# The feed-forward products of an encoder layer as 2x2 blocks with seven block products

## The chip, the cores and the metric

The kernel runs on one core of a Trainium2 chip. The core has a matrix engine (TensorE, "PE" in the profile, with its weight loads as "PEld"), three engines for element work (VectorE "DVE", ScalarE "ACT", GpSimd "POOL"), and a sync engine ("SP") that issues nearly all DMA transfers here. Each engine works through its own instructions in order, and waits on semaphores for the others. PE reads its operands from SBUF and writes its sums to PSUM, which has room here for eight tiles of 128x512 float32 numbers. The metric is the device time of one execution in microseconds.

## The reference

One layer (DEPTH 1, 1024 tokens, D_MODEL 1024). Three token mixers feed gated projections, and the sum goes through `w_out`. After that comes the part that is changed:

```
x  = x + merged @ w_out                  # 1024x1024 @ 1024x1024
h2 = rms_norm(x, norm2_g)
x  = x + (silu(h2 @ ffn_w1) * (h2 @ ffn_w3)) @ ffn_w2
# D_FF = 2816: two products 1024x1024 @ 1024x2816, one 1024x2816 @ 2816x1024
```

All arithmetic is to have float32 accuracy.

## The kernel before

Every matrix operand is split into two parts, a high one of reduced precision ("hi", made by ScalarE with a type conversion) and the remainder ("lo", a subtraction on VectorE), see `split` (L90 to L92). A product is then three matmuls into the same PSUM tile, hi*hi, hi*lo and lo*hi, `mm3` (L94 to L97). Operands that come from DRAM go through `Prep` (L402 to L415): a DMA into a `wr` buffer, the hi part (L413) and the lo part (L414). These run under a raised priority `HP`: a planner in the framework orders the instructions of each engine when the program is built, from priorities and from times that it assumes, so the order of the code and the order on an engine can differ. That order is then fixed. Buffers come from pools: a `tag` has a number of slots, and a new tile waits until the tile that held the slot is no longer used. A pool that is opened where another was closed waits for the tiles that lay at its addresses.

The last third of the kernel has three parts.

The output projection (`out_proj`, L763) works on two halves of 512 tokens. In each it forms four column blocks of 256: per block 4 token tiles x 8 contraction tiles x 3 matmuls of 128x256, from the operand `mT` and prepared `w_out`; then VectorE adds the residual `xr` into `acc` (L777), which holds the whole of x in SBUF until the end. After four blocks, `norm_tile_T` (L417 to L429) computes the RMS norm of the half: ScalarE squares (L422), a short chain for the inverse root (L178 to L187), then for each token tile a scaling on VectorE (L426), 8 transposes on PE (L428) and a split of the transposed tile into h2T.

The feed-forward (`ffn`, L783) goes through 11 groups of 256 hidden columns. In a group, for two column tiles j and two token halves h, there are two PSUM tiles (w1 and w3) of 8 contraction tiles x 3 matmuls of 128x512; then Silu (L800), the product (L801) and a split into `gh`, `gl`, which stay in SBUF. The down projection of the group follows: 8 token tiles x 2 column halves x 2 contraction tiles x 3 matmuls, and VectorE adds each PSUM tile to `acc` (L813). Activations never leave SBUF. The weight buffers hold 2 raw and 8 split tiles.

The output is stored at the end of the last group, one DMA for each token tile.

## Time and profile before

| | |
|---|---|
| median of 3 runs | 2303.83 us (2302.22 to 2306.47) |
| the profiled execution's own time | 2300.59 us |
| its span (first to last instruction) | 2298.8 us |
| mean granted TensorE clock | 0.954 |
| PE busy | 2068.9 us (90%), 10929 matmuls |
| DVE busy | 1274.5 us (55%) |
| ACT busy | 798.4 us (35%) |
| POOL busy | 210.6 us (9%) |
| DMA | 278.51 MB, mean 121 GB/s |

Times within the trace count from the start of the span. The output projection begins at about 1441 us, the feed-forward at 1561 us, and the last result is added at 2294 us. A matmul's record lasts longer than the distance to the next matmul, because matmuls are pipelined: what one costs is the distance from start to start. The page names an idle stretch by the instruction that ended it.

### The profile page before, as it was taken

The numbers are of one execution on the slowest core, as the hardware profiler recorded it, in microseconds if no ns is written. First come the engines' busy times: TensorE is split into PE (matmuls) and PEld (weight loads), VectorE is DVE, ScalarE is ACT, GpSimd is POOL, SyncE is SP. The second block draws the span as 40 slices with busy tenths as digits, with TensorE's granted clock in tenths as the row PEclk, the third lists the DMA queues.
The fourth block names the chain that finished last, engine by engine and source line by source line (L and its number), as shares of the span: only waits on it lengthen the run. The fifth ranks groups of instructions, "written<-read, shape, count | busy, mean of one in ns | idle before, by whom it ended". The sixth has DMA issues, their size and how long they took to land.

```text
span 2298.8 us, 27560 instructions
## 1 busy us (share of the span) xinstructions
PE 2068.9 (90%) x10929; PEld 1735.1 (75%) x10929; DVE 1274.5 (55%) x1977; ACT 798.4 (35%) x1250; POOL 210.6 (9%) x123
## 2 busy tenths in 40 slices
PE   5488989979679998999998799989999999999999
...
PEclk8699999989889999999999999999999999999999
...
GB/s 182 93 208 172 202 143 218 197 248 167 184 169 238 185 174 115 117 67 133 123 137 86 163 84 138 196 114 23 33 55 55 55 37 56 55 27 48 55 19 74
DMA packets 120635, 278.51 MB, mean 121 GB/s; under 512 B 16518, under 2 KB 46712, under 8 KB 118970
## 3 DMA queue, kind: packets, MB, share of 16 engines
...
q0 software_dynamic: 512, 7.34, 0.9%
...
## 4 chain that ended last, share of the span: by engine, by line
PE 63%; DVE 15%; DMA 9%; ACT 6%; issue 3%; POOL 2%; SPq 1%; ACTq 0%; POOLq 0%; DVEq 0%
PE pf L97 11%; PE pf L96 11%; PE pf L95 11%; PE pT L95 4%; PE pT L96 4%; PE pT L97 4%; DVE wlo L414 2%; PE S L631 2%; DMA it<-iv 2%; DMA wraw<-in_w_out 1%; DMA ft<-fw 1%; PE T L645 1%; PE pm L95 1%; PE pm L96 1%; PE pm L97 1%
## 5 line engine op out<-in xcount | busy, mean ns | idle before, releaser
L413 ACT ACTIVATE whi<-wraw 128x512 fp32r<-128x512 f32 (+1 forms) x214 | 168.4, 794 | 476.4 <-PE pf L97 176.6
L414 DVE TENSOR_TENSOR wlo<-wraw,whi 128x512 fp32r<-128x512 f32 (+1 forms) x214 | 208.6, 982 | 222.9 <-ACT whi L413 215.5
L97 PE MATMUL pf<-h2T,wlo 128*128 128x512 f32 x704 | 280.4, 398 | 0.0
L96 PE MATMUL pf<-h2T,whi 128*128 128x512 f32 x704 | 277.8, 395 | 0.0
L95 PE MATMUL pf<-h2T,whi 128*128 128x512 f32 x704 | 276.4, 393 | 0.0
L95 PE MATMUL pT<-hT,whi 128*128 128x512 f32 x576 | 235.0, 408 | 14.0 <-DVE u L450 11.0
L96 PE MATMUL pT<-hT,whi 128*128 128x512 f32 x576 | 232.1, 403 | 0.8 <-DVE hT L92 0.8
L97 PE MATMUL pT<-hT,wlo 128*128 128x512 f32 x576 | 231.9, 403 | 0.0
L801 DVE TENSOR_TENSOR si<-si,pf 128x512 f32<-128x512 f32 x44 | 30.2, 687 | 306.1 <-PE pf L97 305.9
L95 PE MATMUL pN<-whi,hT 128*128 128x256 f32 x576 | 164.8, 287 | 14.0 <-DVE vl L92 8.1
L813 DVE TENSOR_TENSOR acc<-acc,pf 128x512 f32<-128x512 f32 x176 | 119.3, 687 | 96.7 <-PE pf L97 96.6
L96 PE MATMUL pN<-wlo,hT 128*128 128x256 f32 x576 | 164.8, 286 | 1.7 <-DVE wlo L414 1.7
L97 PE MATMUL pN<-whi,hT 128*128 128x256 f32 x576 | 164.1, 285 | 0.0
L96 PEld LDWEIGHTS pf<-h2T,whi 128*128 128x128 f32 x704 | 132.1, 188 | 33.9
L95 PEld LDWEIGHTS pf<-h2T,whi 128*128 128x128 f32 x704 | 132.3, 188 | 31.8
L97 PEld LDWEIGHTS pf<-h2T,wlo 128*128 128x128 f32 x704 | 132.2, 188 | 30.5
L95 PEld LDWEIGHTS pT<-hT,whi 128*128 128x128 f32 x576 | 110.8, 192 | 41.1 <-issue 11.0
L96 PE MATMUL pf<-wlo,gh 128*128 128x512 f32 x352 | 137.1, 390 | 0.0
L95 PE MATMUL pf<-whi,gh 128*128 128x512 f32 x352 | 137.1, 390 | 0.0
L97 PE MATMUL pf<-whi,gl 128*128 128x512 f32 x352 | 136.9, 389 | 0.0
L96 PEld LDWEIGHTS pT<-hT,whi 128*128 128x128 f32 x576 | 110.8, 192 | 26.0 <-DVE hT L92 1.3
L97 PEld LDWEIGHTS pT<-hT,wlo 128*128 128x128 f32 x576 | 110.4, 192 | 24.4 <-issue 0.2
...
## 6 DMA issues: line engine op xcount, KB each, us to landing
...
```

The lines of the kernel that those rows point to most:

```text
L95: nc.tensor.matmul(p,lh,rh,start=first,stop=False)
L96: nc.tensor.matmul(p,lh,rl,start=False,stop=False)
L97: nc.tensor.matmul(p,ll,rh,start=False,stop=last)
L413: nc.scalar.activation(hi,raw,AF.Identity)
L414: (self.lo_eng or nc.vector).tensor_tensor(lo,raw,hi.bitcast(F32),op=ALU.subtract)
L631: nc.tensor.matmul(S[:,512*n:512*n+512],q[:,c,128*t:128*t+128],k[i][:,c,512*n:512*n+512],start=i==0,stop=i==1)
L645: for i in range(4): nc.tensor.transpose(T[:,i,:],e[:,512*n+128*i:512*n+128*i+128],E.ident)
L801: V.tensor_tensor(si,si,P[1],op=ALU.mult)
L813: V.tensor_tensor(acc[:,t,512*d:512*d+512],acc[:,t,512*d:512*d+512],p,op=ALU.add)
```

## The change

The up projection is computed on 2x2 blocks. The normed tokens are cut into two halves of tokens and two halves of the contraction, A11, A12, A21, A22; the weight columns into tile i and tile 11+i and the same two halves of the contraction, B11, B12, B21, B22. With S1=A21+A22, S2=S1-A11, S3=A11-A21, S4=A12-S2, and T1=B12-B11, T2=B22-T1, T3=B22-B12, T4=T2-B21, the four result blocks come from seven block products A11*B11, A12*B21, S4*B22, A22*T4, S1*T1, S2*T2, S3*T3 and seven additions, instead of eight products. This is done for w1 and w3 side by side: a pair of PSUM tiles per product, 2 x 4 contraction tiles x 3 matmuls = 24 matmuls of 128x512.

- `out_proj` loads x into `acc` (now 512 tokens, two slots, of which one becomes `raw0`, the unsplit transposed first half), squares each block as it is done, stores the residual to DRAM (`E.res`), and in the second half forms S1 to S4 and A22 in place of a plain split. The S tiles (`ms`) take the place of `mT`. Between the last block and the second norm, `meanwhile` puts the first two block products of the first group.
- `ffn_up` runs 11 iterations. Each loads four weight tiles, forms T1 to T4 on VectorE, splits seven weight tiles, and combines the PSUM pairs on VectorE and ScalarE into C11, C12, C21, C22. From the gated activations g11, g12, g21, g22 GpSimd forms s1 to s4, and seven 256 KB tiles are stored to DRAM (`E.gs`).
- `ffn_down` runs seven jobs, one for each block product of the down projection. A job goes through 11 contraction tiles in six spans: it loads the activation operand from `E.gs`, splits it, forms the weight combination in place where there is one, splits that, and runs 4 token tiles x 3 matmuls for each contraction tile. Raw `ffn_w2` is loaded into the space of A1 and S, the residual into the space of A22 and a new pool; each job's PSUM is added to the residual tiles, and results are stored as they are complete.

```diff
     def __init__(self,pool,bufs): self.pool,self.bufs=pool,bufs
     def tile(self,shape,dt,tag=None,name=None):
         return self.pool.tile(shape,dt,tag=tag,name=name or tag,bufs=self.bufs.get(tag,1))
+class Either:
+    def __init__(self,p,q): self.p,self.n={0:p,1:q},{}
+    def tile(self,shape,dt,tag=None,name=None):
+        if tag not in ("wh","wl"): return self.p[0].tile(shape,dt,tag=tag,name=name)
+        self.n[tag]=n=self.n.get(tag,1)^1
+        return self.p[n].tile(shape,dt,tag=tag,name=name)
 def split(nc,hi,lo,src,eng=None):
     nc.scalar.activation(hi,src,AF.Identity)
...
                 for h in range(2): split(nc,mT[h][0][:,D],mT[h][1][:,D],gt[:,512*h:512*h+512],nc.gpsimd)
         yield 2.7
-def out_proj(tc,nc,E,prep,a,pool,big,mT,acc,x):
+def out_proj(tc,nc,E,prep,a,pool,big,biga,mT,x,meanwhile):
     V=nc.vector
     g=pool.tile([128,1024],F32,tag="n2g",name="n2g"); dma(nc,g,a['norm2_g'].broadcast_to([128,1024]))
-    h2=[]
+    A1=[biga.tile([128,8,512],F32R,tag="a1",name="A1") for _ in range(2)]
+    A2=[biga.tile([128,4,512],F32R,tag="a2",name="A22") for _ in range(2)]
+    S=None
     for h in range(2):
+        acc=pool.tile([128,4,1024],F32,tag="acc",name="acc")
+        dma(nc,acc,x[512*h:512*h+512].rearrange("(t p) c -> p t c",p=128))
         for c in range(4):
             W=[prep([(lambda v:v,a['w_out'][c][:,4*q:4*q+4,:])],4,256) for q in range(2)]
             p=E.pg.tile([128,4,256],F32,tag="g",name="pw")
             for t in range(4):
+                s=slice(128*t,128*t+128)
                 for k in range(8):
+                    mm3(nc,p[:,t],mT[h][0][:,k,s],mT[h][1][:,k,s],W[k//4][0][:,k%4],W[k//4][1][:,k%4],k==0,k==7)
+            av=acc[:,:,256*c:256*c+256]
+            V.tensor_tensor(av,av,p,op=ALU.add)
+            if c==0: ssq=pool.tile([128,4,4],F32,tag="ssq",name="ssq")
+            for i in range(4):
+                junk=pool.tile([128,4,128],F32,tag="t22",name="junk")
+                nc.scalar.activation(junk[:,0:2],acc[:,i,256*c:256*c+256].rearrange("p (a b) -> p a b",b=128),AF.Square,accum_out=ssq[:,i,c:c+1])
+        dma(nc,E.res[h],acc)
+        if h: meanwhile(A1)
+        st=pool.tile([128,4],F32,tag="sst",name="sst")
+        V.tensor_reduce(st,ssq,axis=AX.X,op=ALU.add)
+        rs=rsqrt_inplace(nc,pool,st,1.0/1024,1e-6,[128,4],"ssr")
+        if h==0: raw=pool.tile([128,8,512],F32,tag="acc",name="raw0")
+        else: S=[big.tile([128,4,4,512],F32R,tag="ms",name="S") for _ in range(2)]
+        for i in range(4):
+            s=slice(128*i,128*i+128)
+            xn=pool.tile([128,1024],F32,tag="xn",name="xn")
+            V.scalar_tensor_tensor(xn,acc[:,i],rs[:,i:i+1],g,op0=ALU.mult,op1=ALU.mult)
+            p=E.px.tile([128,8,128],F32,tag="x",name="ptr")
+            for k in range(8): nc.tensor.transpose(p[:,k,:],xn[:,128*k:128*k+128],E.ident)
+            if h==0:
+                nc.scalar.copy(raw[:,:,s],p)
+                split(nc,A1[0][:,:,s],A1[1][:,:,s],p)
+            else:
+                t=pool.tile([128,4,128],F32,tag="t22",name="t22"); nc.scalar.copy(t,p[:,4:8])
+                x1=pool.tile([128,2,4,128],F32,tag="xn",name="s12"); x3=pool.tile([128,2,4,128],F32,tag="xn",name="s34")
+                V.tensor_tensor(x1[:,0],p[:,0:4],t,op=ALU.add)
+                V.tensor_tensor(x1[:,1],x1[:,0],raw[:,0:4,s],op=ALU.subtract)
+                V.tensor_tensor(x3[:,0],raw[:,0:4,s],p[:,0:4],op=ALU.subtract)
+                nc.gpsimd.tensor_tensor(x3[:,1],raw[:,4:8,s],x1[:,1],op=ALU.subtract)
+                split(nc,S[0][:,0:2,:,s],S[1][:,0:2,:,s],x1)
+                split(nc,S[0][:,2:4,:,s],S[1][:,2:4,:,s],x3)
+                split(nc,A2[0][:,:,s],A2[1][:,:,s],t,nc.gpsimd)
+    return A2,S
+def seven(nc,p,B,A):
+    for k in range(4): mm3(nc,p,B[0][:,k],B[1][:,k],A[0][:,k],A[1][:,k],k==0,k==3)
+def ffn_first(tc,nc,E,a,pool,i,A1):
+    X=E.pg.tile([128,2,512],F32,tag="g",name="f1")
+    R,B=[],[]
+    for w,n in enumerate(('ffn_w1','ffn_w3')):
+        with tc.high_priority(HP):
+            raw=pool.tile([128,8,128],F32,tag="wr",name="wraw"); dma(nc,raw,a[n][i])
+            b=[pool.tile([128,8,128],F32R,tag=t,name="whi") for t in ("wh","wl")]
+            split(nc,b[0],b[1],raw)
+        R.append(raw); B.append(b)
+        seven(nc,X[:,w],[m[:,0:4] for m in b],[m[:,0:4] for m in A1])
+    return X,R,B
+def ffn_second(nc,ps,B,A1):
+    Z=ps.tile([128,2,512],F32,tag="g",name="f2")
+    for w in range(2): seven(nc,Z[:,w],[m[:,4:8] for m in B[w]],[m[:,4:8] for m in A1])
+    return Z
+def ffn_up(tc,nc,E,a,r1,rt,rb,pool,ps,st,A1,A2,S):
+    V=nc.vector
+    Sx=[[m[:,j] for m in S] for j in range(4)]
+    TT=lambda o,x,y,op: V.tensor_tensor(o,x,y,op=op)
+    P=lambda o,x,y,op: nc.gpsimd.tensor_tensor(o,x,y,op=op)
+    c=lambda nm: pool.tile([128,2,512],F32,tag="c",name=nm)
+    new=lambda ps: ps.tile([128,2,512],F32,tag="g",name="fp")
+    def cut(src):
+        with tc.high_priority(HP):
+            b=[rb.tile([128,2,4,128],F32R,tag=t,name="bh") for t in ("bh","bl")]
+            split(nc,b[0],b[1],src)
+        return b
+    def pair(ps,src,A):
+        b=cut(src); p=new(ps)
+        for w in range(2): seven(nc,p[:,w],[m[:,w] for m in b],A)
+        return p
+    def act(t,o=None,u=None):
+        o=t[:,0] if o is None else o
+        nc.scalar.activation(o,t[:,0],AF.Silu)
+        TT(o,o,t[:,1],ALU.mult)
+        return o
+    for i in range(11):
+        (X,R,B),Z=st
+        with tc.high_priority(HP):
+            r2=rt.tile([128,2,8,128],F32,tag="r2",name="r2")
+            for w,n in enumerate(('ffn_w1','ffn_w3')): dma(nc,r2[:,w],a[n][11+i])
+            t1=rt.tile([128,2,4,128],F32,tag="tt",name="t1"); t2=rt.tile([128,2,4,128],F32,tag="tt",name="t2")
+            for w in range(2): TT(t1[:,w],r2[:,w,0:4],R[w][:,0:4],ALU.subtract)
+            TT(t2,r2[:,:,4:8],t1,ALU.subtract)
+        U=c("U"); nc.scalar.copy(U,X)
+        if Z is None: Z=ffn_second(nc,ps,B,A1)
+        C11=c("C11"); TT(C11,U,Z,ALU.add)
+        p6=pair(E.pg,t2,Sx[1]); TT(U,U,p6,ALU.add)
+        g11=act(C11); dma(nc,E.gs[0][:,i],g11)
+        p5=pair(ps,t1,Sx[0]); C12=c("C12"); TT(C12,U,p5,ALU.add)
+        with tc.high_priority(HP):
+            t3=rt.tile([128,2,4,128],F32,tag="tt",name="t3")
+            TT(t3,r2[:,:,4:8],r2[:,:,0:4],ALU.subtract)
+        p7=pair(E.pg,t3,Sx[2]); TT(U,U,p7,ALU.add)
+        C22=c("C22"); TT(C22,U,p5,ALU.add)
+        p3=pair(ps,r2[:,:,4:8],Sx[3]); TT(C12,C12,p3,ALU.add)
+        g22=act(C22); dma(nc,E.gs[6][:,i],g22)
+        with tc.high_priority(HP):
+            for w in range(2): TT(t2[:,w],R[w][:,4:8],t2[:,w],ALU.subtract)
+        p4=pair(E.pg,t2,A2)
+        g12=act(C12); dma(nc,E.gs[1][:,i],g12)
+        if i<10: st=ffn_first(tc,nc,E,a,r1,i+1,A1),None
+        TT(U,U,p4,ALU.add)
+        g21=act(U,pool.tile([128,512],F32,tag="s",name="g21"))
+        s1,s2,s3,s4=(pool.tile([128,512],F32,tag="s",name="s") for _ in range(4))
+        P(s1,g21,g22,ALU.add); dma(nc,E.gs[2][:,i],s1)
+        P(s3,g11,g21,ALU.subtract); dma(nc,E.gs[3][:,i],s3)
+        P(s2,s1,g11,ALU.subtract); dma(nc,E.gs[4][:,i],s2)
+        P(s4,g12,s2,ALU.subtract); dma(nc,E.gs[5][:,i],s4)
+def ffn_down(tc,nc,E,a,r1,rb,big,biga,pool,ps,out):
+    V=nc.vector
+    w2=a['ffn_w2'][0]
+    span=[(j,min(2,11-j)) for j in range(0,11,2)]
+    with tc.high_priority(HP):
+        a1=[biga.tile([128,8,512],F32,tag="a1",name="w2a") for _ in range(2)]
+        ms=[big.tile([128,16,512],F32,tag="ms",name="w2b") for _ in range(2)]
+        flat=[(a1[0],0),(a1[0],2),(a1[0],4),(a1[0],6),(a1[1],0),(a1[1],2)]
+        place={(0,0):flat,(1,0):[(ms[0],j) for j,_ in span],(0,1):[(ms[1],j) for j,_ in span],
+               (1,1):[(ms[0],11),(ms[0],13),(ms[1],11),(ms[1],13),(a1[1],3),(a1[1],5)]}
+        B={}
+        for k,n in ((0,0),(1,0),(0,1),(1,1)):
+            B[k,n]=[t[:,o:o+m] for (t,o),(_,m) in zip(place[k,n],span)]
+            for t,(j,m) in zip(B[k,n],span):
+                r=1408*k+128*j
+                dma(nc,t,w2[r:r+128*m,512*n:512*n+512].rearrange("(m p) c -> p m c",p=128))
+    R=[[pool.tile([128,4,512],F32,tag=f"R{h}{n}",name="R") if h+n else biga.tile([128,4,512],F32,tag="a2",name="R") for n in range(2)] for h in range(2)]
+    U=biga.tile([128,4,512],F32,tag="a2",name="U2")
+    for h in range(2):
+        for n in range(2): dma(nc,R[h][n],E.res[h][:,:,512*n:512*n+512])
+    def add(d,x): V.tensor_tensor(d,d,x,op=ALU.add)
+    def done(h,n,t):
+        r=512*h+128*t.start
+        dma(nc,out[r:r+256,512*n:512*n+512].rearrange("(t p) c -> p t c",p=128),R[h][n][:,t])
+    def sub(o,x,y): return lambda j,m: V.tensor_tensor(B[o][j][:,0:m],B[x][j][:,0:m],B[y][j][:,0:m],op=ALU.subtract)
+    def p1(t,p): nc.scalar.copy(U[:,t],p); add(R[0][0][:,t],p)
+    def p2(t,p): add(R[0][0][:,t],p); done(0,0,t)
+    def p5(t,p): add(R[0][1][:,t],p); add(R[1][1][:,t],p)
+    def p7(t,p): add(R[1][0][:,t],p); add(R[1][1][:,t],p)
+    def p6(t,p):
+        add(U[:,t],p)
+        for h,n in ((1,1),(0,1),(1,0)): add(R[h][n][:,t],U[:,t])
+        done(1,1,t)
+    def p3(t,p): add(R[0][1][:,t],p); done(0,1,t)
+    def p4(t,p): add(R[1][0][:,t],p); done(1,0,t)
+    jobs=((0,(0,0),None,p1),(1,(1,0),None,p2),
+          (2,(0,0),sub((0,0),(0,1),(0,0)),p5),
+          (3,(0,1),sub((0,1),(1,1),(0,1)),p7),
+          (4,(0,0),sub((0,0),(1,1),(0,0)),p6),
+          (5,(1,1),None,p3),
+          (6,(0,0),sub((0,0),(1,0),(0,0)),p4))
+    for n,(g,b,form,post) in enumerate(jobs):
+        P=[(ps if n%2 else E.pg).tile([128,2,512],F32,tag="g",name="fo") for _ in range(2)]
+        for i,(j0,m) in enumerate(span):
+            with tc.high_priority(HP):
+                raw=r1.tile([128,2,512],F32,tag="wr",name="graw"); dma(nc,raw[:,0:m],E.gs[g][:,j0:j0+m])
+                A=[r1.tile([128,2,512],F32R,tag=t,name="gA") for t in ("wh","wl")]
+                split(nc,A[0][:,0:m],A[1][:,0:m],raw[:,0:m])
+                if form: form(i,m)
+                W=[rb.tile([128,2,512],F32R,tag=t,name="w2h") for t in ("bh","bl")]
+                split(nc,W[0][:,0:m],W[1][:,0:m],B[b][i][:,0:m])
+            for jj in range(m):
+                for t in range(4):
                     s=slice(128*t,128*t+128)
...
+                    mm3(nc,P[t//2][:,t%2],A[0][:,jj,s],A[1][:,jj,s],W[0][:,jj],W[1][:,jj],j0+jj==0,j0+jj==10)
+        for t in range(2): post(slice(2*t,2*t+2),P[t])
 def encoder(tc,a,out):
     nc=tc.nc
...
+        E.res=[D(f"res{h}",[128,4,1024]) for h in range(2)]
+        E.gs=[D(f"gs{i}",[128,11,512]) for i in range(7)]
...
         pst.close()
         with ExitStack() as cc:
             E.pg=pool(cc,"pg5",{'g':4},space=PSUM)
-            big=pool(top,"big",{'big':4},side="right")
-            mT=[[big.tile([128,8,512],F32R,tag="big",name="mT") for _ in range(2)] for _ in range(2)]
+            top_big=ExitStack(); big=pool(top_big,"big",{'ms':2},side="right")
+            mm=[big.tile([128,2,8,512],F32R,tag="ms",name="mT") for _ in range(2)]
+            mT=[[m[:,h] for m in mm] for h in range(2)]
             for _ in merge(nc,E,prep,a,mo,2,macc,False,mT): pass
         mst.close(); wst.close()
         with ExitStack() as cc:
-            prep=Prep(tc,E,pool(cc,"wpc",{'wr':2,'wh':8,'wl':8}))
-            acc=pool(cc,"acc").tile([128,8,1024],F32,tag="acc",name="acc")
+            biga=pool(top_big,"biga",{'a1':2,'a2':2},side="right")
+            r1=pool(cc,"wpc",{'wr':3,'wh':2,'wl':2})
+            E.pg=pool(cc,"pg4",{'g':2},space=PSUM)
+            st=[]
             with ExitStack() as c2:
-                E.pg=pool(c2,"pg4",{'g':2},space=PSUM)
                 E.px=pool(c2,"px4",{'x':2},space=PSUM)
-                h2=out_proj(tc,nc,E,prep,a,pool(c2,"op",{'xr':2,'xn':2,'ssr':3,'ssq':2}),big,mT,acc,x)
+                prep=Prep(tc,E,Either(r1,pool(c2,"wpo",{'wh':2,'wl':2})))
+                def meanwhile(A1):
+                    f=ffn_first(tc,nc,E,a,r1,0,A1)
+                    st.append(((f,ffn_second(nc,E.pg,f[2],A1)),A1))
+                A2,S=out_proj(tc,nc,E,prep,a,pool(c2,"op",{'xn':3,'ssr':3,'ssq':2,'acc':2,'t22':1}),big,biga,mT,x,meanwhile)
+            ps=pool(cc,"pf",{'g':2},space=PSUM)
+            rt=pool(cc,"rt",{'r2':1,'tt':2})
+            rb=pool(cc,"rb",{'bh':3,'bl':3})
             with ExitStack() as c3:
-                ps=pool(c3,"pf",{'f':4,'f2':4},space=PSUM)
-                ffn(tc,nc,E,prep,a,pool(c3,"fp",{'si':2,'gh':6,'gl':6}),ps,h2,acc,out)
+                up=pool(c3,"fp",{'c':4,'s':5})
+                ffn_up(tc,nc,E,a,r1,rt,rb,up,ps,st[0][0],st[0][1],A2,S)
+            with ExitStack() as c3:
+                ffn_down(tc,nc,E,a,r1,rb,big,biga,pool(c3,"fd"),ps,out)
+        top_big.close()
...
     for n in ('w_oa','w_ob','w_oc'): t[n]=column_tiles(x[n][0],128)
-    for n in ('w_out','ffn_w1','ffn_w3'): t[n]=column_tiles(x[n][0],256)
+    t['w_out']=column_tiles(x['w_out'][0],256)
+    for n in ('ffn_w1','ffn_w3'): t[n]=column_tiles(x[n][0],128)
```

40 lines of the change are left out of this document (removed).

## The prediction

> **What bounds the kernel now.** I read the page first, then the span cut at the borders of the last third (output projection, the gap after it, feed-forward, tail), then the groups and the waits of these parts.
>
> ```profile
> PE   5488989979679998999998799989999999999999
> PEclk8699999989889999999999999999999999999999
> ...
> 1440.00:1543.50 103.50, 98.71 (x800) 97.89 (x800) 46.46 (x43) 33.58 (x37) 3.15 (x2) 0.96 0.51 158
> 1543.50:1561.00 17.50, 7.18 (x33) 6.41 (x33) 12.11 (x15) 8.60 (x13) 0.00 (x0) 0.62 0.20 60
> 1561.00:2294.20 733.20, 733.12 (x3170) 594.71 (x3169) 248.09 (x324) 115.11 (x148) 0.00 (x0) 1.00 0.14 46
> 2294.20:2298.80 4.60, 0.00 (x0) 0.00 (x0) 0.65 (x1) 0.00 (x0) 0.00 (x0) 0.97 0.29 118
> ```
>
> The columns after the stretch are its length and the busy time of PE, PEld, DVE, ACT and POOL, then clock, DMA share and GB/s. For 733.2 us PE never pauses and the clock is full; VectorE is busy 34% of it and the DMA engines 14%. So the feed-forward takes what its matmuls take, and removing matmuls there removes time as long as the others keep up.
>
> ```profile
> L97 PE MATMUL pf<-h2T,wlo 128*128 128x512 f32 x704 | 280.4, 398 | 0.0
> L96 PE MATMUL pf<-h2T,whi 128*128 128x512 f32 x704 | 277.8, 395 | 0.0
> L95 PE MATMUL pf<-h2T,whi 128*128 128x512 f32 x704 | 276.4, 393 | 0.0
> L96 PE MATMUL pf<-wlo,gh 128*128 128x512 f32 x352 | 137.1, 390 | 0.0
> L95 PE MATMUL pf<-whi,gh 128*128 128x512 f32 x352 | 137.1, 390 | 0.0
> L97 PE MATMUL pf<-whi,gl 128*128 128x512 f32 x352 | 136.9, 389 | 0.0
> ```
>
> 3 x 704 + 3 x 352 = 3168 matmuls of one shape, 733.2 / 3168 = 0.2314 us from one to the next (the 0.39 us of a record overlaps its neighbours).
>
> **Removed: an eighth of the matmuls.** The up projection falls from 11 x 192 = 2112 to 11 x 7 x 24 = 1848, the down projection from 1056 to 7 x 11 x 12 = 924. That is 396 matmuls of the same shape: 396 x 0.2314 = **-91.6 us**. Both operands keep 128 columns held and 512 moving, so I keep the price.
>
> **Added: the gap before the S operands.** The second norm is the one place where PE now stands open.
>
> ```profile
> 1544.38 1.22 DVE L777 TENSOR_TENSOR acc<-pw,xr 128x1024 f32<-128x1024 f32 x1
> ...
> 1549.99 0.17 DVE L178 TENSOR_SCALAR rsa<-ssq 128x4 f32<-128x4 f32 x1 [3.26 <-ACT junk L422]
> ...
> 1551.23 2.48 DVE L426 SCALAR_TENSOR_TENSOR xn<-acc,rsy,n2g 128x1024 f32<-128x1024 f32 x2
> ...
> L414 DVE TENSOR_TENSOR wlo<-wraw,whi 128x1024 fp32r<-128x1024 f32 x82 | 100.6, 1237 | 111.1 <-ACT whi L413 111.0
> L413 ACT ACTIVATE whi<-wraw 128x1024 fp32r<-128x1024 f32 x82 | 85.8, 1058 | 297.7 <-PE pf L97 176.6 <-DMA wraw<-in_w_out 38.2 <-DMA wraw<-in_ffn_w 30.0
> L801 DVE TENSOR_TENSOR si<-si,pf 128x512 f32<-128x512 f32 x44 | 30.2, 687 | 306.1 <-PE pf L97 305.9
> L426 DVE SCALAR_TENSOR_TENSOR xn<-acc,rsy,n2g 128x1024 f32<-128x1024 f32 x8 | 10.0, 1281 | 0.9 <-PE ptr L428 0.9
> L119 ACT ACTIVATE sc<-fg 128x256 f32<-128x256 f32 x16 | 6.0, 408 | 26.3 <-DVE fg L111 24.7 <-DVE y L494 1.6
> L92 POOL TENSOR_TENSOR mT<-gt,mT 128x512 fp32r<-128x512 f32 x16 | 25.5, 1622 | 29.2 <-ACT mT L91 29.2
> L92 POOL TENSOR_TENSOR mT<-gt,mT 128x512 fp32r<-128x512 f32 x4 | 6.9, 1760 | 4.2 <-ACT mT L91 4.2
> ...
> L414 DVE TENSOR_TENSOR wlo<-wraw,whi x2: 1271/1780/2289, 1440.8 to 1441.9; 128x1024 fp32r<-128x1024 f32 x2
> ```
>
> Count from the last matmul of the projection. The add takes 1.2, the last four squares of 256 elements about 0.4 each and some 0.2 to read each sum, the short chain 1549.99 to 1551.23, so 1.2: about 5.5 us in all. Then VectorE has for each token tile one scaling (1.28), three 512-element operations (3 x 0.69) and two 1024-element splits (2 x 1.24): 5.8 us. GpSimd has two 512-element operations for each tile, 1.6 us each. The last row is two splits while GpSimd ran such an operation: one took 2.29 instead of 1.27, so I add 1.0 for each of the two: 7.9 us a tile, 31.4 for four, and 3 for the first transposes and copies. The S2 product can begin at about 40 us. `meanwhile` gives PE 48 matmuls, 11.1 us, in that time. So 29 us are lost where 17.5 are lost now: **+11.4**. Between: with no interference and no start-up, 5.5 + 23.3 - 11.1 - 17.5 = 0; with GpSimd's operations entirely in series (8 x 1.76, the mean beside the splits of 1440) and the first group's four weight splits ahead on VectorE, about +22. I take the middle, which the 2.29 supports.
>
> The Trainium skill (SBUF — State Buffer, two separate sides) goes further: VectorE with two SBUF inputs and GpSimd hold a shared port pair exclusively, the loser waits for the whole instruction. By that rule it would be 1.6 and not 1.0 for each, some +5 us here. The row agrees with a wait, but two splits can't show that it is always whole.
>
> **Added: x is reloaded for the second half.** The slot of `acc` is free only when the residual is stored (2.1 MB) and the last tile is scaled.
>
> ```profile
> 1443.00:1461.00 18.00, 18.00 (x146) 18.00 (x145) 5.41 (x5) 4.24 (x4) 0.15 (x1) 0.94 0.68 215
> 10.00:20.00 10.00, 3.56 (x17) 3.49 (x18) 4.86 (x9) 4.97 (x9) 3.05 (x6) 1.00 0.94 328
> ...
> 1494.68 4.16 ACT junk L422 x8
> ...
> 1509.70 2.48 DVE L426 SCALAR_TENSOR_TENSOR xn<-acc,rsy,n2g 128x1024 f32<-128x1024 f32 x2
> ...
> PE ptr L428 <- DVE xn L426: 12.3, 2, 9.0
> ```
>
> 215 to 328 GB/s are the rates in a mixed and in the fullest stretch. The first half's squares begin at 1494.68, about 1 us after its last matmul, and the last scaling ends at 1512.18, some 18 us after that matmul; 2.1 MB take 6.4 to 9.8 more, the add 1.2: 26 to 29. Meanwhile PE has two blocks of 96 matmuls of 256 columns (103.5 / 768 = 0.135 each with all pauses, 26 us) and the transposes before it needs a PSUM tile back. I take **+2**, from 0 to 12 if the load stands behind weight loads on SP.
>
> **Added: the work of the up loop.** An iteration has 168 x 0.2314 = 38.9 us of PE. VectorE: seven splits 8.7, T1 to T4 5.2 (four 1024-element operations, two of them in halves), seven PSUM combinations of 1024 elements at 1.22 = 8.5, four products 2.75: 25.2 us, with 4 x 1.0 for GpSimd's s1 to s4, 29. ScalarE: seven hi parts 7.4, a copy 1.0, four Silu 2.4: 11. Transfers: four weight tiles of 0.52 MB and seven stores of 0.26 MB, 3.9 MB or 101 GB/s, half of 215. All fits under PE. The order is what can fail: a split queued behind a VectorE addition that waits for PE. Weight splits have three slots, so one may be two products (11 us) late; each PSUM pair rests for two products or more; r2 has one slot, but is free after the S2 product, some 20 us before it is needed again. Behind the last store of an iteration (s4, about 2.6 + 3 x 1.6 after the A22 product) SP holds back the next loads, which have this slack. Below it can't be under 0; above, one hi and lo pair in the open per iteration is 11 x 2.3 = 25. Nearest to what PE does now (no weight wait at all in 733 us): **+5**.
>
> **Added: the work of the down jobs.** A span of 24 matmuls is 5.55 us. VectorE: two splits and, in four jobs, a combination: 3.7; results of a job add at most 9.8 (T2 job: eight additions), while a job lasts 30.5. It fits. The loads are the dispute: 2.9 MB of `ffn_w2` fit under the last iteration, but 8.7 MB and 4.2 MB of residual can start only when S and A22 are free, at the end of it, 12.8 MB: 39 to 60 us at the two rates. If operand loads stand behind all that, five prefetched spans (27 us) cover part, and 12 to 33 us remain; if they go first, nothing. I take **+8**, from 0 to 33.
>
> **Tail.** 4.6 us now; two additions of 1.22 instead of one of 0.69, then a store of the same 512 KB: **+1** (0.5 to 2).
>
> **Sum**, on the profiled execution's own 2300.59 us: -91.6 + 11.4 + 2 + 5 + 8 + 1 = -64.2, so 2236.4. The median of the runs stands 3.2 above this execution: **2240 us**.
>
> **The rivals.**
>
> *The down projection waits for its operands* (12.8 MB ahead of them): +33 instead of +8, 2265. For it: all loads stand in one queue, SP's, and raw w2 has the raised priority and is written first in the code. Against: the first operands exist long before S is free. The Trainium skill (DMA: Bandwidth & Descriptors, Queues, rings and completion order) says that a DMA engine consumes a queue's descriptors in ring order; by it an operand load issued late waits for all 12.8 MB. That would be this rival. The longest wait here,
>
> ```profile
> ACT whi L413 <- DMA wraw<-in_w_out: 38.2, 14, 9.1
> ```
>
> 9.1 us for one of 14 weight tiles of 0.5 MB at 215 GB/s (2.4 us alone), fits a backlog of about 2 MB.
>
> *Everything hides*: gap, reload and both loops at their lower ends, 2300.6 - 91.1 + 3.2 = 2213. For it: 34% VectorE now. Against: the chain for S has twice the VectorE work of the present norm.
>
> *Slower: each group of 24 matmuls ends in a hand-over.* VectorE works in order, and if the planner puts the lo split of the next group behind the addition that frees the last, PE waits one 1.24 us split at each. There are 77 + 38.5 = 115.5 groups: 143 us. The rest of the sum is -77.2, so it decides from 77.2 / 115.5 = 0.67 us a group; at 1.24 the time is 2369. For it: VectorE's share in the loop doubles from 34% to 65-75%, and each PSUM pair is combined in place in chains (U, C12, C22). Against: two products of slack everywhere, and in
>
> ```profile
> DVE wlo L414 <- ACT whi L413: 58.9, 21, 7.9
> PE ptr L428 <- DVE h2T L92: 1.3, 2, 0.9
> ```
>
> (1440 to 1620, and all of PE's waits from 1490 on beside the 12.3 above) VectorE waits for its input and not PE for VectorE. A milder form, 0.3 us a group, gives 2300.6 - 77.2 + 35 + 3.2 = 2262.
>
> **How the numbers follow.** Forecast 0.67, own range 2220 to 2262; starved down projection 0.12; all hidden 0.08; mild hand-over 0.08 (up to 2300); full hand-over, slower, 0.05. About 0.2% (4.6 us) is what can be told from no change. Faster 0.94, same 0.01 (the mild form's end), slower 0.05. The range 2213 to 2276 takes in the lower ends of all terms and both nearer rivals.
>
> **What would show it.** 2772 matmuls of 128x512 after the gap at 0.231 us each: if not, the first term is wrong. The S2 product starting about 40 us after the projection's last matmul, with VectorE and GpSimd nearly full between. No PE idle in the up loop above 0.5 us an iteration. In the first 60 us of the down projection a wait of ScalarE's hi part for the operand load, 8 us on PE's side. In the second half of the projection a VectorE addition that waits for x, 2 us on PE. What would make it wrong most: PE idle at each group, or DMA near its full share at the start of the down jobs.

## The result, and the profile after

The changed kernel takes 2219.08 us (median of 4 runs, 2216.63 to 2221.51), the kernel before 2303.57 us (4 runs, 2302.22 to 2306.47): a ratio of 0.9632, 95% interval 0.9615 to 0.9648. That is 84.5 us less where the prediction had 63.8 less; 2219 lies in its full range (2213 to 2276), 21 us under its value and 1 us under the 2220 to 2262 that it had for its own sum. The profiled execution took 2216.63 us, with a span of 2214.8 us, 84.0 less than the span of before.

First the busy digits of PE and its clock over 40 slices, from the page of the changed kernel, then its last third cut where the stages begin (output projection, gap, both feed-forward loops, tail), with the columns of the prediction's table.

```profile
PE   5479998888958999899999879899699999999999
PEclk8789999998979999999999999999799999999999
...
1440.80:1538.70 97.90, 96.85 (x801) 96.18 (x802) 40.01 (x39) 41.00 (x84) 2.53 (x2) 0.98 0.44 154
1538.70:1578.00 39.30, 18.04 (x82) 14.43 (x80) 33.13 (x37) 18.29 (x29) 12.86 (x8) 0.70 0.21 80
1578.00:2209.50 631.50, 631.37 (x2724) 512.25 (x2724) 397.95 (x390) 197.09 (x215) 56.82 (x44) 1.00 0.37 127
2209.50:2214.80 5.30, 0.00 (x0) 0.00 (x0) 1.22 (x1) 0.00 (x0) 0.00 (x0) 0.84 0.53 198
```

The digit 7 in the PE clock (the 29th slice) is the one place of the last third where PE stands, and it is longer than before. Behind it PE works without a pause through both loops, as it did before, at full clock but for its first eight matmuls, while VectorE's share has risen from 34% to 63% and the DMA engines' from 14% to 37%.

Then the matmuls of the S products and of the down projection by tile (duration in ns, first and last start), and all that PE waited for from 1430 us to the end (us in total, times, longest). The numbers after L are lines of the changed kernel, where `mm3` is L103 to L105, `split` L99 and L100, `Prep` L421 and L422, and the norm in `out_proj` L804 and L806.

```profile
L103 PE MATMUL fp<-S,bh x352: 392/394/796, 1578.1 to 1993.5; 128*128 128x512 f32 x176
...
L103 PE MATMUL fo<-w2h,gA x308: 387/389/394, 1999.8 to 2208.6; 128*128 128x512 f32 x154
...
PE ptr L806 <- DVE xn L804: 13.7, 3, 4.6
PE fp L103 <- ACT bh L99: 7.7, 1, 7.7
PE pw L103 <- ACT whi L421: 4.6, 1, 4.6
PE pw L104 <- DVE wlo L422: 0.9, 1, 0.9
```

None of the four lies behind 1578 us: the first two are the gap, the others stand at the start of the projection. No product of the up loop and none of the down jobs had to wait.

From stage to stage, the two spans compare so (before and after, us; the projection starts at 1440.8 and 1440.9):

| | before | after | moved | forecast |
|---|---|---|---|---|
| projection, to its last matmul | 102.5 | 97.6 | -4.9 | +2 |
| gap, less the matmuls of `meanwhile` in it | 17.7 | 39.4 - 11.2 = 28.2 | +10.5 | +11.4 |
| feed-forward matmuls | 733.0 | 631.3 + 11.2 = 642.5 | -90.5 | -91.6 + 5 + 8 |
| tail | 4.7 | 5.4 | +0.7 | +1 |

Together -84.2. (The 39.4 counts from the end of the projection's last matmul; from its start, as the runs below are compared, it is 39.5.) So the two terms that come from rows of this kernel, the matmuls and the gap, came out within about 1 us; the three that were put in for unknown costs, +15 together, came out as -4.9.

### The profile page after: what moved, and what is told of

The parts are those of the page before. It is cut to its first block, busy times and chain, and to the rows that moved or that the text cites. A ratio compares the mean times of both kernels' runs of the same rounds, so it can differ in the third digit from the quotient of the medians.

```text
span 2214.8 us, 27366 instructions
## 1 busy us (share of the span) xinstructions
PE 1975.1 (89%) x10533; PEld 1658.3 (75%) x10533; DVE 1438.3 (65%) x2061; ACT 897.6 (41%) x1378; POOL 281.6 (13%) x175
## 4 chain that ended last, share of the span: by engine, by line
PE 66%; DVE 14%; DMA 8%; ACT 5%; issue 4%; POOL 3%; SPq 1%; POOLq 0%; ACTq 0%; DVEq 0%
PE fp L104 5%; PE fp L103 5%; PE fp L105 5%; PE pT L103 4%; PE pT L104 4%; PE pT L105 4%; PE fo L105 3%; PE fo L103 3%; PE fo L104 3%; DMA it<-iv 3%; PE f L104 2%; PE f L103 2%; PE f L105 2%; PE S L639 2%; PE pm L104 2%
## 5 line engine op out<-in xcount | busy, mean ns | idle before, releaser
L103 PE MATMUL pT<-hT,whi 128*128 128x512 f32 x576 | 235.5, 409 | 14.4 <-DVE u L458 11.0
L105 PE MATMUL pT<-hT,wlo 128*128 128x512 f32 x576 | 232.7, 404 | 0.0
L422 DVE TENSOR_TENSOR wlo<-wraw,whi 128x512 fp32r<-128x512 f32 (+1 forms) x148 | 130.0, 885 | 152.2 <-ACT whi L421 144.4
L421 ACT ACTIVATE whi<-wraw 128x512 fp32r<-128x512 f32 (+1 forms) x148 | 99.3, 676 | 207.4 <-PE pT L104 114.2
L103 PE MATMUL pN<-whi,hT 128*128 128x256 f32 x576 | 164.9, 287 | 14.6 <-DVE vl L100 8.3
L105 PE MATMUL pN<-whi,hT 128*128 128x256 f32 x576 | 164.1, 285 | 0.0
L103 PE MATMUL fp<-S,bh 128*128 128x512 f32 x352 | 139.6, 397 | 7.7 <-ACT bh L99 7.7
L103 PEld LDWEIGHTS pT<-hT,whi 128*128 128x128 f32 x576 | 111.4, 193 | 40.9 <-issue 10.3
L104 PE MATMUL fp<-S,bh 128*128 128x512 f32 x352 | 141.1, 401 | 0.0
L105 PE MATMUL fp<-S,bh 128*128 128x512 f32 x352 | 138.3, 393 | 0.0
L105 PEld LDWEIGHTS pT<-hT,wlo 128*128 128x128 f32 x576 | 111.0, 193 | 24.5 <-issue 0.2
L103 PEld LDWEIGHTS pN<-whi,hT 128*128 128x128 f32 x576 | 110.9, 193 | 16.3 <-issue 8.5
L105 PE MATMUL fo<-w2h,gA 128*128 128x512 f32 x308 | 119.8, 389 | 0.0
L104 PE MATMUL fo<-w2h,gA 128*128 128x512 f32 x308 | 119.8, 389 | 0.0
L103 PE MATMUL fo<-w2h,gA 128*128 128x512 f32 x308 | 119.7, 389 | 0.0
L103 PE MATMUL X<-rh,ft 128*128 128x256 f32 x256 | 77.9, 304 | 46.5 <-ACT rh L99 41.2
L104 PEld LDWEIGHTS pN<-wlo,hT 128*128 128x128 f32 x576 | 110.9, 193 | 1.3 <-DVE wlo L422 1.3
L105 PEld LDWEIGHTS pN<-whi,hT 128*128 128x128 f32 x576 | 111.1, 193 | 0.0
L99 ACT ACTIVATE bh<-t 128x1024 fp32r<-128x1024 f32 x44 | 46.6, 1061 | 145.9 <-PE fp L104 138.1
```

What stands on the lines that cost most here:

```text
L99: nc.scalar.activation(hi,src,AF.Identity)
L103: nc.tensor.matmul(p,lh,rh,start=first,stop=False)
L104: nc.tensor.matmul(p,lh,rl,start=False,stop=False)
L105: nc.tensor.matmul(p,ll,rh,start=False,stop=last)
L421: nc.scalar.activation(hi,raw,AF.Identity)
L422: (self.lo_eng or nc.vector).tensor_tensor(lo,raw,hi.bitcast(F32),op=ALU.subtract)
```

## The experiments

The kernels are the changed kernel with the edits shown, but for the fifth, which is the kernel before with one edit. The front of the program, which nobody changed, ends a few us earlier or later in each execution (the projection's first matmul lies between 1437.3 and 1448.1 us), so stages are compared from that point on.

### One half of the change at a time

In the first run only the up projection has seven products; the down projection has eight, from the same stored activations.

```diff
-    jobs=((0,(0,0),None,p1),(1,(1,0),None,p2), ... (6,(0,0),sub((0,0),(1,0),(0,0)),p4))
+    jobs=[((0,1,2,6)[2*h+k],(k,n),(h,n),k) for h in range(2) for n in range(2) for k in range(2)]
-        P(s1,g21,g22,ALU.add); dma(nc,E.gs[2][:,i],s1)
-        ...
+        dma(nc,E.gs[2][:,i],g21)
```

> The changed kernel with the down projection as eight block products (two jobs accumulate into one PSUM block; g21 is stored in place of s1 to s4, and no weight combinations are formed); the up projection keeps its seven. Theory (PE is the only bound, each matmul is worth its distance of 0.2318 us): 132 matmuls come back, +30.6 us on 2219.1, so 2249.7, with no PE wait in either loop. Rival (part of the gain came from cheaper operand handling in the down jobs, or the seven-product down form hides stalls): the step is smaller, 10 to 20 us, or PE waits show up in the down jobs.

It took 2249.2 us (2246.96 to 2250.59), a ratio of 0.9772, interval 0.9752 to 0.9792. From the projection's first matmul to the last of the down projection there are 797.9 us, where the changed kernel has 768.2: 29.7 more, for 132 matmuls more. That is 0.225 us for each. In both runs the matmuls of the down projection stand 0.227 us apart (those of the up projection 0.233; 0.2318 is the mean over both loops), so it is the price of a matmul and nothing besides. The up loop gains nothing by not forming s1 to s4 (416.1 us from its first S product to its last, 415.9 in the changed kernel), and the combinations of the down jobs cost nothing.

In the second run only the down projection has seven products. The up projection has eight, so the second half of the tokens goes through the plain norm and split, and no S is formed.

```diff
-                x1=pool.tile(...); x3=pool.tile(...)
-                ... (S1 to S4, their splits, A22's split)
+                split(nc,S[0][:,0:2,:,s],S[1][:,0:2,:,s],p.rearrange("p (a b) c -> p a b c",b=4))
```

> The changed kernel with the up projection as eight block products (four PSUM pairs of 48 matmuls an iteration, four weight splits, no T or S operands, the second half normed with a plain split); the down projection keeps its seven. Theory (the S chain is what holds the gap open): 264 matmuls come back, +61.2, and the 28.2 us that PE now loses before the first product of the second half fall to 3 to 8: 2255 to 2260. Rival (the gap is held open by the first group's weight splits, whose buffers lie where the projection's pool was): the loss stays near 28 and the time is 2280.

2261.21 us (2260.16 to 2261.3), ratio 0.9824, interval 0.9805 to 0.9844. First to last matmul 809.4 us, 41.2 more than the changed kernel: 264 matmuls more are 61.2, so 20 us came back. They came back in the gap. PE's timeline there has only these pauses (in brackets, with what ended them):

```profile
1556.41 2.72 PE L805 MATMUL ptr<-ident,xn 128*128 128x128 f32 x16 [1.73 <-DVE S L100]
1559.53 0.79 PE L103 MATMUL fp<-A,bh 128*128 128x512 f32 x1 [0.40 <-ACT bh L99]
1560.98 0.79 PE L105 MATMUL fp<-A,bh 128*128 128x512 f32 x1 [0.23 <-DVE bh L100]
...
1565.30 0.39 PE L103 MATMUL fp<-S,whi 128*128 128x512 f32 x1
```

Where the changed kernel has no product to do from 1550 to 1578 us, this one begins its third 18 us after its last projection matmul (1541.4). From the end of the projection to the first product of the second half, at 1565.3 us, it takes 23.7 us with 61 matmuls in them (the 48 of `meanwhile` and 13 of the next block), 14.1 us at full clock, so 9.6 us are lost instead of 28.2. The 9.6 include PE's first matmuls behind the pause, at half clock; in the changed kernel these cost 1.7 us more, behind the 28.2. The sums of the activations, then, cost 28.2 + 1.7 - 9.6 = 20.3 us in the open, which is what came back. The seven products of the up projection save 61.2 for that. The theory had 3 to 8 us for the loss and 2260 at most for the time, so both came out a little above it; the rival, with 28 and 2280, is far off.

### Why the projection became shorter

The prediction had +2 us here for the reload of x, and 4.9 us went away. Two edits came into question: the squares of the norm, which are now taken after each column block, and the number of raw weight slots, three instead of two. The third run takes the squares after the last block, as before.

```diff
-            for i in range(4): ... AF.Square,accum_out=ssq[:,i,c:c+1])      # after each block
+        for i in range(4):                                                 # after the last
+            nc.scalar.activation(junk,acc[:,i],AF.Square,accum_out=ssq[:,i:i+1])
```

> The changed kernel with the squares of each half taken after its fourth block, four of 1024 elements as before the change, instead of block by block. Theory (the earlier squares are why the projection got 4.9 us shorter): PE waits for the first norm's transposes again, +4.9 there, and the second norm's chain begins 2.5 later: 2226. Rival (the third raw buffer and the whole-half x loads did it): only the 2.5 of the second norm, 2221.5.

2215.88 us (2211.13 to 2223.02), ratio 0.9633, interval 0.9609 to 0.9658. The projection takes 1437.3 to 1534.0, 96.7 us, and the first S product follows 39.5 us later, as in the changed kernel. The early squares buy nothing, in the projection or in the gap. Both forecasts had the gap longer without them; why it is not is seen below, under what sets the gap.

The fifth run is the kernel before with a third raw slot.

```diff
-            prep=Prep(tc,E,pool(cc,"wpc",{'wr':2,'wh':8,'wl':8}))
+            prep=Prep(tc,E,pool(cc,"wpc",{'wr':3,'wh':8,'wl':8}))
```

> The kernel before, with one edit: three raw slots instead of two for the weights of the last pool (the changed kernel has three; the edit takes 4 KB more and changes nothing else). Read from the stage: first to last matmul of the output projection, 102.5 us before and 97.6 us after the change. Theory (the output projection got 4.9 us shorter because a late w_out load no longer holds ScalarE's queue ahead of the first half's norm): the stage takes 96.5 to 98.5 us, the three-microsecond wait of the transposes for VectorE's scaled rows is gone, and the whole is about 2299 us (2296 to 2302). Rival (the gain has to do with the new order of work in the changed kernel: raw copy, blocks, no second norm): the stage stays at 102 to 103 us and the whole at 2303 to 2304 us.

2298.29 us (2292.92 to 2303.56), ratio to the kernel before 0.9979, interval 0.9968 to 0.999. What happens is seen on ScalarE in the kernel before, at the end of the first half. Its hi parts (L413) come in order ahead of the squares (L422), and wait for their weights:

```profile
1489.53 1.06 ACT L413 ACTIVATE whi<-wraw 128x1024 fp32r<-128x1024 f32 x1 [3.06 <-DMA wraw<-in_w_out]
1493.62 1.06 ACT L413 ACTIVATE whi<-wraw 128x1024 fp32r<-128x1024 f32 x1 [3.04 <-DMA wraw<-in_w_out]
1494.59 1.04 ACT L422 ACTIVATE junk<-acc 128x1024 f32<-128x1024 f32 x1
```

So a weight that the second half needs holds up the norm of the first, its transposes come late, and PE has nothing. The same stretches (10 us each, matmuls and transposes counted behind the PE time) first of before, then of the run with three slots:

```profile
1440.80:1450.80 10.00, 9.27 (x63) 8.98 (x64) 3.43 (x2) 0.92 (x2) 2.35 (x2) 0.78 0.66 206
1490.80:1500.80 10.00, 8.44 (x72) 8.23 (x70) 3.91 (x6) 7.15 (x12) 0.00 (x0) 1.00 0.59 181
1500.80:1510.80 10.00, 8.27 (x57) 8.27 (x58) 8.63 (x9) 3.62 (x4) 0.00 (x0) 0.83 0.21 57
```

```profile
1440.80:1450.80 10.00, 9.24 (x51) 8.95 (x52) 6.32 (x5) 4.30 (x5) 2.42 (x2) 0.62 0.65 194
1490.80:1500.80 10.00, 10.00 (x85) 9.81 (x84) 5.31 (x10) 6.86 (x12) 0.00 (x0) 1.00 0.47 157
1500.80:1510.80 10.00, 10.00 (x86) 9.70 (x86) 10.00 (x9) 5.75 (x6) 0.00 (x0) 1.00 0.34 107
```

With three slots the norm costs PE nothing (85 and 86 instead of 72 and 57). The whole stage is 99.1 us (the theory had 96.5 to 98.5), 3.4 less than before and not 4.9; the missing 1.5 lie in the first row: PE's clock stayed lower after the pause ahead of the projection (0.62 against 0.78), and 12 matmuls fewer at 0.117 us are 1.4. Two other runs bear that out: the changed kernel's projection takes 99.0 and 99.1 us in the fourth and tenth run, where the clock stayed at 0.50 for 7.3 and 7.5 us behind its first matmul (7.5 in the fifth), and 96.7 to 97.8 in all others, where it did so for 4.2 to 4.5. So the third slot accounts for the 4.9: 3.4 are shown on the kernel before by itself, and the rest is what the later clock took back there.

### What sets the gap

The gap is VectorE's: from 1551.60 us until the first weight split of the S products at 1577.32 it hardly pauses. One token tile of the changed kernel, and the end of the chain, in VectorE's timeline (start, us):

```profile
1546.14 1.29 DVE L804 SCALAR_TENSOR_TENSOR xn<-acc,rsy,n2g 128x1024 f32<-128x1024 f32 x1
...
1558.71 0.68 DVE L813 TENSOR_TENSOR s<-ptr,t 128x512 f32<-128x512 f32 x1
1559.31 0.68 DVE L815 TENSOR_TENSOR s<-raw,ptr 128x512 f32<-128x512 f32 x1
1559.91 0.68 DVE L814 TENSOR_TENSOR s<-s,raw 128x512 f32<-128x512 f32 x1
1560.51 1.28 DVE L804 SCALAR_TENSOR_TENSOR xn<-acc,rsy,n2g 128x1024 f32<-128x1024 f32 x1
1561.71 3.55 DVE L100 TENSOR_TENSOR S<-s,S 128x1024 fp32r<-128x1024 f32 x2
1565.18 0.68 DVE L813 TENSOR_TENSOR s<-ptr,t 128x512 f32<-128x512 f32 x1
...
1577.32 2.35 DVE L100 TENSOR_TENSOR bh<-t,bh 128x1024 fp32r<-128x1024 f32 x2
```

A tile takes 6.47 us (1558.71 to 1565.18). The two splits in a row take 3.55, where two weight splits later take 2.35. Beside them runs GpSimd:

```profile
L100 DVE TENSOR_TENSOR S<-s,S 128x1024 fp32r<-128x1024 f32 x8 | 13.1, 1635 | 1.3 <-ACT S L99 1.1
...
L816 POOL TENSOR_TENSOR s<-raw,s 128x512 f32<-128x512 f32 x4 | 7.8, 1945 | 2.8 <-DVE s L814 2.8
L100 POOL TENSOR_TENSOR A<-t,A 128x512 fp32r<-128x512 f32 x4 | 5.1, 1268 | 116.0 <-ACT A L99 116.0
```

What the chain starts with is PE's. The first scaled row is ready at 1547.43 us, but its transposes stand on PE behind the 48 matmuls of `meanwhile`, and follow them without a wait:

```profile
1549.85 1.04 PE L806 MATMUL ptr<-ident,xn 128*128 128x128 f32 x8
```

So the matmuls that fill the gap also hold back, by 2.4 us, the chain that ends it. That is why the late squares of the third run cost nothing: there the row is ready 1.6 us later behind the projection (1544.47, the projection's last matmul at 1533.98), and still ahead of the end of `meanwhile` at 1545.30; the first tile's sums begin 13.0 us behind the projection's last matmul in that run and 13.1 in the changed kernel. No run here puts the transposes first.

The fourth run gives GpSimd's two operations per tile to VectorE.

```diff
-                nc.gpsimd.tensor_tensor(x3[:,1],raw[:,4:8,s],x1[:,1],op=ALU.subtract)
+                V.tensor_tensor(x3[:,1],raw[:,4:8,s],x1[:,1],op=ALU.subtract)
-                split(nc,A2[0][:,:,s],A2[1][:,:,s],t,nc.gpsimd)
+                split(nc,A2[0][:,:,s],A2[1][:,:,s],t)
```

> The changed kernel with GpSimd's two operations of each token tile in the S chain moved to VectorE. Theory (VectorE is full there, 6.47 us a tile, 1.19 of it waiting for GpSimd): the two operations cost 1.2 and the wait goes, so no change, 2219 within 1.5, and the S splits last 1.22 again. Rival 1 (the long splits have another cause): 1.2 us a tile on top, 2224. Rival 2 (the chain waits for GpSimd's 2.2 us result, not for VectorE): 1 us a tile less, 2215.

2225.92 us (2220.69 to 2229.89), ratio 0.967, interval 0.9648 to 0.9693; the first S product is 43.9 us behind the projection instead of 39.5. (Another 1.4 us of the time are its projection, see above.) Its tile on VectorE:

```profile
1570.22 0.68 DVE L100 TENSOR_TENSOR A<-t,A 128x512 fp32r<-128x512 f32 x1
1570.82 0.69 DVE L816 TENSOR_TENSOR s<-raw,s 128x512 f32<-128x512 f32 x1
1571.43 1.23 DVE L100 TENSOR_TENSOR S<-s,S 128x1024 fp32r<-128x1024 f32 x1
...
1576.64 0.69 DVE L813 TENSOR_TENSOR s<-ptr,t 128x512 f32<-128x512 f32 x1 [1.66 <-ACT t L811]
```

The splits did get short, 1.22 us each: GpSimd's operations do stretch VectorE's. But two more operations take 1.2 us a tile, and now VectorE waits 1.6 us a tile for ScalarE's copy of the transposes, so that a tile takes 8.2 us. The time agrees with the rival, the mechanism with the theory; the order in which a tile's work comes matters as much as the length of its operations.

### How much slack the two loops have

The prediction gave 5 us to the up loop, up to 25, and 8 to the start of the down projection, up to 33. Both came out at nothing. How near was that? The seventh run has two pairs of buffers for split operands instead of three.

```diff
-            rb=pool(cc,"rb",{'bh':3,'bl':3})
+            rb=pool(cc,"rb",{'bh':2,'bl':2})
```

> The changed kernel, with two buffer pairs instead of three for the split weight operands of the up loop and of the down projection. It tests how much slack the up loop has, to which the prediction gave 5 us and up to 25. Theory (a pair of products is 24 matmuls of 0.2318 us, 5.6 us, and a cut is 1.0 us of ScalarE and 1.2 us of VectorE: the cut has the length of a whole product to be made in, so the third buffer buys nothing): no PE wait in either loop, 2217 to 2222 us. Rival (the loop holds only because cuts run two products ahead): PE waits 0.5 to 1.5 us at many of the 54 or so products behind forms of VectorE, 25 to 60 us in all, 2245 to 2280 us.

2222.32 us (2219.74 to 2224.5), ratio 0.9645, interval 0.9631 to 0.9659. The up loop takes 416.3 us from its first S product to its last (415.9 with three pairs), the down jobs 212.4 (209.3). So a weight split in the up loop is ready with a whole product to spare. In the down projection the third pair is worth 3 us, which the theory did not have, in short waits of PE's weight loads for VectorE's split.

The eighth run issues each load of the down projection's weights twice.

```diff
-                dma(nc,t,w2[r:r+128*m,512*n:512*n+512].rearrange("(m p) c -> p m c",p=128))
+                for _ in range(2): dma(nc,t,w2[r:r+128*m,512*n:512*n+512].rearrange("(m p) c -> p m c",p=128))
```

> The changed kernel, with every load of the down projection's weights issued twice into the same place: 23.0 MB instead of 11.5 MB ahead of, and in one queue with, the down projection's other operands. Nothing else changes. It tests the rival of the prediction that priced a starved down projection at 33 us, and how far from it the kernel is. Theory (the queue has slack: the loads go at 386 GB/s, are through soon after the first operands are used up, and the fourth group of operands of the first job, needed about 15 us after the job starts, comes some 12 us early): 11.5 MB more at 386 GB/s is 30 us more in the queue, so that group lands late and PE stands 15 to 20 us once, in the first job, with nothing later; time 2237 us (2230 to 2245). Rival 1 (the slack is a multiple of that, operands pass the loads): no PE wait, 2217 to 2222 us. Rival 2 (the kernel already is at the edge): PE stands 27 to 33 us, 2246 to 2252 us.

2253.34 us (2249.96 to 2255.25), ratio 0.978, interval 0.9763 to 0.9797: 34 us more, with a pause of the length that the second rival had. PE stands once, in the first job, ahead of its last span; behind the pause the next 24 matmuls take 8.1 us instead of 5.4, at half clock. From the waits and SP's timeline of this run (start, and how long the issues of the group took):

```profile
PE fo L103 <- ACT gA L99: 30.6, 1, 30.6
...
1996.22 47.48 SPq L83 DMA_DIRECT2D w2b<-in_ffn_w  x31
...
2055.14 5.75 SPq L83 DMA_DIRECT2D graw<-gs  x4
```

And the issue of the same operand loads in the changed kernel:

```profile
1994.18 14.95 SPq L83 DMA_DIRECT2D w2b<-in_ffn_w  x16
2010.17 10.57 SPq L83 DMA_DIRECT2D graw<-gs  x3
```

The down projection's first matmul stands at 1999.8 us in the changed kernel and 2001.9 here. So the issue moved from 10.4 to 53.2 us behind the start of the job, 42.9 us for 11.5 MB more (269 GB/s for what was added, and not the 386 on which the expectation rested; all traffic from 1980 to 2056 us went at 305), and PE waited 30.6 of them. The slack of the changed kernel is 42.9 - 30.6 = 12.3 us, as the theory had it, so it is not at the edge; what the theory got wrong is the rate of the queue. The rival of the starved down projection did not come, but it was 12 us away.

### Starting with S1

If the gap is the length of VectorE's chain up to the first product's operand, a shorter chain closes it. The remaining runs make the first product S1*T1 instead of S2*T2, and form only S1 ahead of it: S3 = A11 - A21 takes A11's place, S2 is A22 - S3, S4 is A12 - S2, and their splits come later. In the first of these GpSimd still makes S2, S4 and a part of A22, and the operands have two buffer pairs.

```diff
+                    V.tensor_tensor(x1,p[:,0:4],t,op=ALU.add)                             # S1
+                    V.tensor_tensor(raw[:,0:4,s],raw[:,0:4,s],p[:,0:4],op=ALU.subtract)   # S3
+                    split(nc,S[0][:,0,:,s],S[1][:,0,:,s],x1)
+                nc.gpsimd.tensor_tensor(t2,t,raw[:,0:4,s],op=ALU.subtract)                # S2
+                nc.gpsimd.tensor_tensor(raw[:,4:8,s],raw[:,4:8,s],t2,op=ALU.subtract)     # S4
...
+    return r2,t1,t2,pair(ps,t1,[m[:,0] for m in S]),pair(ps,t2,[m[:,1] for m in S])
-            rb=pool(cc,"rb",{'bh':3,'bl':3})
+            rb=pool(cc,"rb",{'bh':2,'bl':2})
```

> The changed kernel, with the sums of the activations formed in another order: for each token tile only S1 = A21 + A22 and its two parts stand ahead; S3 = A11 - A21 is kept in the place of A11, S2 is taken as A22 - S3 and S4 as A12 - S2 on GpSimd, and the parts of S3 and S4 are cut after the cuts of the first weight operands. The first iteration begins with the S1 product, then S2, and the weight cuts have two buffer pairs instead of three. Same result, no work left out. Theory (the 28 us that PE loses before the sums' products is the length of VectorE's chain up to the first product's operand): VectorE has about 17.5 us of work ahead of the first product (4 norms at 1.2, 4 additions and 4 subtractions at 0.65, 8 splits of 512 columns at 0.62, 1 of 1024 and one weight cut at 1.2 each) where it had 27, so the first product starts 29 to 32 us after the projection's last matmul, not 39.5, and what was moved behind lies beside the first two products (11 us of PE); time 2210 us (2206 to 2214). Rival 1 (the moved splits only change place: the S3 product waits for them as long): the first product is early, but PE then waits 7 us or more ahead of the third, and the time is 2217 to 2221. Rival 2 (two buffer pairs for the weight cuts are too few in the up loop): PE waits about 1 us at many of the 55 products and the time is over 2225.

2218.56 us (2216.39 to 2223.43), ratio 0.9632, interval 0.9616 to 0.9648: no gain, although the first product came as forecast, 31.8 us behind the projection. VectorE beside GpSimd, then PE at its first products, in this run's timelines:

```profile
1557.20 0.68 DVE L816 TENSOR_TENSOR raw<-raw,ptr 128x512 f32<-128x512 f32 x1
1558.32 1.21 DVE L100 TENSOR_TENSOR S<-acc,S 128x512 fp32r<-128x512 f32 x1 [0.44 <-ACT S L99]
1559.45 1.75 DVE L100 TENSOR_TENSOR S<-s,S 128x512 fp32r<-128x512 f32 x1
...
1571.57 0.79 PE L103 MATMUL fp<-S,bh 128*128 128x512 f32 x1 [11.60 <-ACT bh L99]
...
1574.45 0.80 PE L105 MATMUL fp<-S,bh 128*128 128x512 f32 x1 [1.15 <-DVE bh L100]
...
1578.46 0.63 PE L105 MATMUL fp<-S,bh 128*128 128x512 f32 x1
1578.89 0.63 PE L103 MATMUL fp<-S,bh 128*128 128x512 f32 x1
...
1580.06 0.40 PE L103 MATMUL fp<-S,bh 128*128 128x512 f32 x1
```

Two things took the 7.7 us back. PE came out of its pause at half clock: matmuls 0.43 us apart until 1580.06, 16 of them where the changed kernel has about 8 (the windows show 0.50 from 1578 to 1581), 1.6 us, and the pause of 1.15 in the first product. By the last S product the lead is 4.7 us. Then the down projection takes 212.4 instead of 209.3, as in the run with two buffer pairs, and 1.6 remain. The time is that of the first rival, but not by its mechanism: the S3 product did not wait.

The next run takes GpSimd out of the chain, holds everything but S1 and S3 back behind the last S1 part, and gives the down projection a third pair of buffers from a new pool.

```diff
-                nc.gpsimd.tensor_tensor(t2,t,raw[:,0:4,s],op=ALU.subtract)
+    with tc.issue_after(seen.ins), tc.high_priority(HP):      # seen: the last part of S1
+        for s,t,t2 in rest:
+            V.tensor_tensor(t2,t,raw[:,0:4,s],op=ALU.subtract)
...
+                ffn_down(tc,nc,E,a,r1,Thirds(rb,pool(c3,"rb3")),big,biga,pool(c3,"fd"),ps,out)
```

> The order of the run that forms S1 first, with three edits: GpSimd takes no part before the products (its three operations a token tile go to VectorE), nothing but S1, S3 in place and their cuts may stand on VectorE ahead of the last S1 part, and the down projection has its third pair of buffers again (the up loop keeps two, for which it showed no wait). In the run before, VectorE's parts of 512 columns took 1.2 to 1.75 us beside GpSimd and 0.68 alone, and 39.5 us between the projection's last matmul and the first product became 31.9. Theory (the gap is VectorE's chain up to the first product's operand, GpSimd's stretching of it included): first scaled row 7.6 us after the last matmul, 4 of them and one cut 6 us, four tiles at 3 times 0.68 us and about 0.5 us of waiting each 10 us, the weight cut on both engines 2.2 us: first product 25 to 28 us after, some 12 us earlier than in the changed kernel; 2 to 4 us of it are lost again at the fourth product, since everything else of the sums stands behind; 2210 us (2206 to 2214). Rival (PE's granted clock, 0.50 after the idle time, comes back only some 6 to 10 us after PE is busy again, or later the earlier PE starts, so an early start runs at half speed): first product as early, but the time is 2214 to 2219.

2226.96 us (2225.63 to 2233.96), ratio 0.9686, interval 0.9663 to 0.9709: slower than the changed kernel, with the first product where the theory had it, at 25.6 us. A split of 512 columns of S is now 0.69 us; the lost time has two lines of its own in the waits:

```profile
PE fo L111 <- DVE w2h L107: 8.2, 1, 8.2
PE fp L110 <- ACT U L919: 7.5, 1, 7.5
...
PE fo L110 <- ACT w2h L106: 2.8, 1, 2.8
```

Both are places in SBUF. The copy U of the first pair lies where the rows of the second half lie, free only after the last part of A22; the third pair lies where the up loop's C tiles lay, free only at its end. The theory had not looked at where the tiles lie.

The run sent with it scales the rows in two steps, with the norm's weight on VectorE during the projection and the row's factor on ScalarE.

```diff
+                V.tensor_tensor(av,av,g[:,256*c:256*c+256].unsqueeze(1).broadcast_to([128,4,256]),op=ALU.mult)
-            V.scalar_tensor_tensor(xn,acc[:,i],rs[:,i:i+1],g,op0=ALU.mult,op1=ALU.mult)
+            nc.scalar.activation(xn,acc[:,i],AF.Copy,scale=rs[:,i:i+1])
```

> The same as the run with GpSimd out of the chain, with one more edit in the second half: the rows before the sums are scaled in two steps, by the weight of the norm on VectorE block by block during the projection (each block's result is stored first), and by the row's own factor on ScalarE, which has half of this stretch free. Same result. Theory (VectorE's chain sets the gap): four operations of 1.2 us leave it, three of the four multiplications hide under the projection and the fourth under the wait for the row sums, so the first product starts 3 to 5 us earlier than without the edit; 2206 us (2202 to 2211). Rival (ScalarE is the next bound: it gets four operations of 1.0 us more in front of copies and cuts that VectorE waits for): the first product starts within 1 us of the other run's, 2209 to 2213 us.

2228.05 us (2223.03 to 2229.52), ratio 0.9679, interval 0.9659 to 0.9698, with the same two waits. The first product stands at 24.1 us, 1.5 earlier than beside it: between theory and rival, and the time is no better.

The last run mends the two places: U of the first iteration goes to a free raw slot, the third pair lies under the rows and serves both loops, and S4 is split ahead of A22.

```diff
-        U=c("U"); nc.scalar.copy(U,X)
+        U=c("U") if i else r1.tile([128,2,512],F32,tag="wr",name="U")
+        with tc.high_priority(0 if i else HP): nc.scalar.copy(U,X)
...
+            th=Thirds(rb,pool(cc,'rbx'))
```

> The order of the two runs before (S1 first, GpSimd out of the chain), with what made them slow taken away. In them PE lost 7.5 us to the copy of the first product pair out of PSUM, whose place in SBUF came free only with the last cut of A22, and 11 us to the down projection's third pair of buffers, whose place came free only when the up loop's buffers did. Here the copy goes to a free raw slot of the weights in the first iteration, the third pair of buffers lies under the sums' rows and serves both loops, and S4 is cut ahead of A22. Theory (the gap is VectorE's chain up to the first product's operand, and what stands behind fits beside the next four products): first product 25 to 27 us after the projection's last matmul (39.4 in the changed kernel), 1 to 4 us lost at the third and fourth products, 3 us more at half clock, both loops else without waits; from the last matmul of the projection to the end of the span 665 to 670 us where the changed kernel has 676.3; time 2210 us (2206 to 2214). Rival (VectorE's whole work on the sums sets the time, wherever it stands: what is started early is lost at the third to fifth product): 673 us or more, 2215 to 2221 us.

2213.29 us (2210.57 to 2222.85), ratio 0.9622, interval 0.9595 to 0.9649. Neither of the two waits is left. From the projection's last matmul to the end of the span it takes 670.0 us where the changed kernel has 676.3. The first product is 24.7 us behind the projection, 14.9 earlier, and 8.6 of that are lost again by the last S product:

```profile
PE fp L110 <- DVE C L891: 5.5, 1, 5.5
...
1584.00:1587.00 3.00, 0.00 (x0) 0.00 (x0) 3.00 (x6) 0.00 (x0) 0.00 (x0) 0.78 0.05 18
1587.00:1592.00 5.00, 3.05 (x7) 2.04 (x8) 4.96 (x5) 2.97 (x3) 0.00 (x0) 0.50 0.00 0
```

At the fourth product PE waits 5.5 us for a PSUM pair that VectorE, full in these rows, has still to read, and that pause brings half clock once more. So the theory and its rival share the result: the chain ahead of the first product sets when PE starts, and VectorE's whole work on the sums sets how much of an early start is kept. In its stages this version is 6 us better than the changed kernel; by the intervals of the whole time the two can't be told apart.

## Why the prediction was right or wrong

**Removed matmuls** (forecast -91.6): right. The two loops run 2724 matmuls in 631.4 us, 0.2318 each, against 0.2314 assumed; the difference, 1.1 us in all, is within the 1.7 us that the first eight lose at half clock. The price is a mean of 0.233 (up) and 0.227 (down), and served because both loops lose an eighth of theirs. Each half of the change, run alone, shows no second price.

**The gap** (+11.4, measured +10.5; S2 product forecast at 40 us, measured 39.4): the sum was right and its parts were not, so its closeness is luck. The first tile's sums begin 12.9 us behind the end of the projection (1551.60 against 1538.66) and not 5.5 + 3 = 8.5: the scaling came after 7.5 us and not 5.5, but what counted is that the transposes stood behind the 11.2 us of `meanwhile`. From there to the first S product, four tiles and the last splits, it took 26.5 us (6.47 for a tile) and not 31.4. GpSimd's interference was charged at 1.0 us for each of eight operations. Measured it is 8 x (1.635 - 1.22) = 3.3 us on the splits and 4 x (0.866 - 0.69) = 0.7 on L814. The Trainium skill's rule of one exclusive holder (SBUF — State Buffer, two separate sides), which would have made the charge 1.6, is borne out: in the S1 run the operations with one input in PSUM keep 0.68 us and only those with both in SBUF grow; and in the changed kernel a tile's two splits take 3.55 us instead of 2.35, longer by 1.2 where GpSimd's operation takes 1.26 alone. That operation itself begins while VectorE scales a row, and takes 1.945 on the mean. (The 1.6 of the forecast was such a mean too, with the waiting in it.) So what failed in the charge is the count: in most tiles only one of GpSimd's two operations meets VectorE operations with both inputs in SBUF.

**Reload of x** (+2, with the stage at -4.9): the step that failed. The reload itself is hidden, PE does not wait for it. But the stage was taken to stay as it was, and the diff's line with three raw slots instead of two was not priced, although the 38.2 us for which ScalarE waited for `w_out` were on the table, among the rivals of another stage (3.3 us in the changed kernel). The run of the kernel before with three slots shows this cause alone.

**Up loop** (+5, up to 25) and **down jobs** (+8, up to 33): the mechanisms were looked for and did not occur; charges for an unknown order were put into the sum, where the rows at hand (busy shares, slots) all said that it fits. The up loop has a whole product of slack. The operand that held PE up in the run with doubled loads comes 12.3 us early in the changed kernel. The sign that was looked for, a hi part of the first job that waits for its operand, is not there; the one wait for a transfer is 2.0 us of VectorE for the residual, off PE's path. The rate behind the 33 us, 215 to 328 GB/s, fits: in the run with doubled loads the queue gave 269 for what was added.

**Tail** (+1): +0.7.

**The rivals.** The starved down projection did not come, and what would bring it is measured: 12 us more in the queue. A hand-over price of VectorE at each group did not come, mild or full: not one wait in 2724 matmuls. "Everything hides" (2213, chance 0.08) is nearest to the measured 2219, nearer than the forecast itself, apart from the gap, which did not hide, and the projection, which gained. The errors of the sum, 6.9 + 5 + 8 with the other terms cancelling, are the 20 us between 2236.4 and the 2216.6 of the profiled execution.
